# Adding the experts' results to the residual rows in DRAM by accumulating scatters

## The chip, the cores and the metric

The kernel runs on one core of a Trainium2 chip. The metric is the device time of one execution in microseconds (us). Before the change it was 1234.18 us, the median of 3 runs (1233.81 to 1234.71).

## The reference, cut to what matters

One decoder layer on 1024 tokens of width 1024, all in float32. A mixing layer (dilated attention and a convolution) gives `x1`; then a mixture of experts adds to it, and a last norm gives the output:

```python
x = x + gt1 * mix                                   # x1
h2 = rms_norm(x, g_norm2) * (1.0 + sc2) + sh2
x = x + gt2 * hier_moe(h2, ...)                     # 32 experts, each token goes to 2 of them
return rms_norm(x, g_final)

# hier_moe, per token t and its two experts e:
#   out[t] += w[t, e] * ((silu(h2[t] @ w_gate[e]) * (h2[t] @ w_up[e])) @ w_down[e])
```

So 2048 rows of 1024 float32 (4 KB each) come out of the experts, two for each token, and each token's two rows are added to its row of `x1` before the last norm.

## The kernel before, in words

The first half of the kernel (up to about 590 us) computes the modulation, the projections, the convolution, the attention, the output projection and the router. In `second_norm` each block of 128 tokens writes its normed rows to the DRAM tensor `h2d` and its residual rows to the DRAM tensor `x1d` (L799, L800). `tables` (L869) turns the router's choice into columns of indices: `ti` is the token of each slot of an expert, `si` is the row of the result buffer of that slot (twice the token, plus 0 or 1 for the token's first or second expert), and `ws` is the weight. Slots that are empty get an index out of bounds, and no row is moved for them.

The second half works through the experts in order. Each has 6 MB of weights (`gate`, `up`, `down`, 2 MB each), loaded by the SP queue (`stage_w`, `eload`, L598) in two 1 MB loads for each into a ring of eight 2 MB buffers, in order of use; a load waits until the buffer's last reader is done. For an expert of 128 slots, `stage_gu` splits each weight into a high and a low part (the ACT cast L931 and the VectorE subtraction L932) and multiplies in three passes (L997 to L999), `stage_h` transposes, and `stage_d` multiplies by `down` (L1065 to L1067). The twelve experts of `PK` have 64 slots and use plain float32 matmuls on the loaded weights (`gu_halves` L977, `d_halves` L1043). One expert, `XP`, is computed for a second block of slots as well. That makes 33 blocks.

GpSimd's queue (POOL) carries, in program order, an indirect DMA that gathers a block's rows of `h2d` (`gather`, L918, into one of three buffers `xe`) and an indirect DMA that scatters a block's results (`scatter`, L1029). VectorE writes the results, scaled by `ws` and `gt2`, into one of two buffers `ys` (L1049, L1073). In the kernel before, each result has its own row of a DRAM buffer `ybuf` of 2048 rows, and the scatters are declared free of each other, so that none waits for the one ahead of it.

Behind the experts stands `overflow(0)`: a conditional block (`tc.If`, L1245) for slots that did not fit, on all engines. In this run it is skipped. Then comes the end, a loop over eight blocks of 128 tokens (L1264 to L1278): load both result rows of each token (1 MB a block), add them on GpSimd (L101, called from L1271), add `x1` on VectorE (L1272; `x1d` was loaded ahead of the conditional block, L1237), square and sum on ACT (L1274), root and reciprocal (L1275, L1276), scale (L1277), and store (L1278, issued by ACT). What sets the order of instructions on each engine is the program order with a scheduler that moves ready work forward; each engine and each queue runs its own instructions in order.

Of the kernel before, what the change touches and what calls it, by code (L numbers as in the profile page):

```python
# [9 lines left out]
F32 = mybir.dt.float32  # L10
# [8 lines left out]
T = 1024  # L19
D = 1024  # L20
H = 8
E = 32
# [23 lines left out]
def trunk_kernel(ctx, tc, x, c, w_mod, b_mod, g_norm1, w_in, conv_w, conv_b, conv_ln_g, conv_ln_b,  # L46
# [13 lines left out]
    dram = ctx.enter_context(tc.tile_pool(name="dram", bufs=1, space=DRAM))  # L60

    h2d = dram.tile([T, D], F32, name="h2d")
    ybuf = dram.tile([2 * T, D], F32, name="ybuf")
    x1d = dram.tile([T, D], F32, name="x1d")
    modd = dram.tile([4, D], F32, name="modd")

# [514 lines left out]
    def ring(i):  # L581

        i %= NR
        if i not in rings:
            if i < 5:
                rings[i] = (raw if i < 2 else rawl if i == 2 else mixp).tile([P, 8, 512], F32, name="raw")
            else:
                rings[i] = (wop if i > 5 else att0).tile([P, 8, 512], F32, name="raw", tag=("pT0", "wo6", "wo2")[i - 5])
        return rings[i]
# [248 lines left out]
    for tt in range(2, 8):  # L838
# [3 lines left out]
        if tt % 4 == 3:  # L842
# [11 lines left out]
    wop0.release()  # L854


    early_t, late_t = [[rtc.tile([P, n], dt, name=f"{nm}{n}") for nm, dt in (("ti", I32), ("si", I32), ("ws", F32))]
                       for n in (LO, E - LO + 1 + NOV)]

    half_t = [rtc.tile([P, E - LO], dt, name=f"{nm}h") for nm, dt in (("ti", I32), ("si", I32), ("ws", F32))]  # L860
    tb = rtc.tile([P, 4, 2, E], F32, name="tb")

    def slots(e):

        if e < LO:
            return [t[:, e:e + 1] for t in early_t]
        return [t[:, e - LO:e - LO + 1] for t in (half_t if e in PK else late_t)]

    def tables(tb, dst, pool, halves=False):  # L869

        ti, si, ws = dst
        n = tb.shape[-1]
        em = pool.tile([P, n], F32, name=f"em{n}", bufs=1)
        v.tensor_scalar(em, tb[:, 0, :], 0.0, BIG, op0=OP.is_equal, op1=OP.mult)
        if halves:
            v.scalar_tensor_tensor(em, tb[:, 0, :], -1.0, em, op0=OP.add, op1=OP.add)
            v.tensor_scalar(ti, em, 2.0, upper, op0=OP.mult, op1=OP.add)
            v.scalar_tensor_tensor(em, em, 2.0, tb[:, 1, :], op0=OP.mult, op1=OP.add)
            v.tensor_scalar(si, em, 2.0, upper, op0=OP.mult, op1=OP.add)
        else:  # L880
            v.scalar_tensor_tensor(ti, tb[:, 0, :], -1.0, em, op0=OP.add, op1=OP.add)
            v.scalar_tensor_tensor(em, tb[:, 0, :], -1.0, em, op0=OP.add, op1=OP.add)
            v.scalar_tensor_tensor(si, em, 2.0, tb[:, 1, :], op0=OP.mult, op1=OP.add)
        v.tensor_add(ws, tb[:, 2, :], tb[:, 3, :])

    t0 = wk3.tile([P, 4, LO], F32, name="t0", bufs=1)
# [21 lines left out]
          for i in range(NX)]  # L908
    for t in xe:
        nc.gpsimd.memset(t, 0.0)  # L910
    scat = []

    gat = []

    def gather(e):
# [110 lines left out]
        st["t", e] = hh, hl  # L1026

    def scatter(ys, e, n):
        s = nc.gpsimd.indirect_dma_start(  # L1029
            out=ybuf.rearrange("t (n f) -> (t n) f", n=n),  # L1030
            out_offset=bass.IndirectOffsetOnAxis(ap=slots(e)[1], axis=0),
            in_=ys, in_offset=None, bounds_check=2 * n * T - 1, oob_is_err=False)
        for o in scat:
            tc.declare_no_dep(s.ins, o.ins, reason="each slot has its own row")
        scat.append(s)

    def d_halves(e):
        h2 = st.pop(("t", e))
        wd = wt[e, 2].rearrange("p (k a) f -> p k (a f)", a=2)
        py = psx.tile([P, D], F32, name="py")[:, 0:512]  # L1040
        for k in range(4):
            for g in range(2):
                nc.tensor.matmul(py[64 * g:64 * g + 64, :], h2[:, k % 2, k // 2 * 64:k // 2 * 64 + 64],  # L1043
                                 wd[:, k, 512 * g:512 * g + 512], start=(k == 0), stop=(k == 3),
                                 skip_group_check=True)
        ys = moe.tile([P, D], F32, name="ys")[:, 0:512]
        for g in range(2):
            ps = slice(64 * g, 64 * g + 64)
            nc.vector.scalar_tensor_tensor(ys[ps], py[ps], slots(e)[2][ps], gt2b[ps, 512 * g:512 * g + 512],  # L1049
                                           op0=OP.mult, op1=OP.mult)  # L1050
        scatter(ys, e, 2)

    def stage_d(*es):
        if es[0] in PK:
            return d_halves(es[0])
        hs = [st.pop(("t", e)) for e in es]
        wd = wt[es[0], 2]
        py = psx.tile([P, D], F32, name="py")
        py = [[py[:, 0:512], py[:, 512:1024]]]
        if len(es) > 1:  # L1060
            py.append([psg.tile([P, F], F32, name=nm) for nm in ("pg", "pu")])
        for k, hi, lo in wparts(wd, DP):
            for (hh, hl), o2 in zip(hs, py):
                for half, o in enumerate(o2):
                    nc.tensor.matmul(o, hh[:, k, :], hi[:, half, :], start=(k == 0), stop=False)  # L1065
                    nc.tensor.matmul(o, hh[:, k, :], lo[:, half, :], start=False, stop=False)  # L1066
                    nc.tensor.matmul(o, hl[:, k, :], hi[:, half, :], start=False, stop=(k == 3))  # L1067
        for e, o2 in zip(es, py):
            ws = slots(e)[2]
            ys = moe.tile([P, D], F32, name="ys")  # L1070
            for half, o in enumerate(o2):
                sl = slice(half * 512, half * 512 + 512)
                nc.vector.scalar_tensor_tensor(ys[:, sl], o, ws, gt2b[:, sl], op0=OP.mult, op1=OP.mult)  # L1073
            scatter(ys, e, 1)
# [156 lines left out]
    stage_w(E)  # L1231
    stage_d(E - 1)


    fx = [ring(i).rearrange("p (t k) f -> p t (k f)", k=2) for i in (0, 1)]
    for i, f in enumerate(fx):
        nc.sync.dma_start(f, x1d[i * 512:i * 512 + 512, :].rearrange("(t p) d -> p t d", p=P))  # L1237
    gfb = ring(7).rearrange("p k f -> p (k f)")[:, 0:D]
    bcast(gfb, g_final[None, :])

# [19 lines left out]
    psx.release()  # L1260


    yv = ybuf.rearrange("(t k) d -> t (k d)", k=2)
    for tt in range(8):  # L1264
        ts = slice(tt * P, (tt + 1) * P)
        if tt % 2 == 0:
            fy = ring((5, 6, 2, 3)[tt // 2]).rearrange("p (t k a) f -> p t k (a f)", t=2, k=2)
        f = fx[tt // 4][:, tt % 4, :]
        y = fy[:, tt % 2]
        nc.sync.dma_start(y.rearrange("p k d -> p (k d)"), yv[ts, :])  # L1270
        gp(y[:, 0, :], y[:, 0, :], y[:, 1, :], OP.add)  # L1271
        nc.vector.tensor_add(f, f, y[:, 0, :])  # L1272
        fs = moe.tile([P, 2], F32, name="fst")
        nc.scalar.activation(y[:, 1, :], f, AF.Square, accum_out=fs[:, 0:1])  # L1274
        nc.scalar.activation(fs[:, 1:2], fs[:, 0:1], AF.Sqrt, scale=1.0 / D, bias=epsc)  # L1275
        nc.vector.reciprocal(fs[:, 1:2], fs[:, 1:2])  # L1276
        nc.vector.scalar_tensor_tensor(y[:, 0, :], f, fs[:, 1:2], gfb, op0=OP.mult, op1=OP.mult)  # L1277
        nc.scalar.dma_start(out[ts, :], y[:, 0, :])  # L1278
    moe.release()
    tabp.release()  # L1280
    wop.release()
# [57 lines left out]
```

## Time and profile before

| | before |
|---|---|
| median of 3 runs | 1234.18 us |
| the profiled execution | 1230.17 us |
| its span in the trace | 1228.4 us |
| granted TensorE clock, mean | 0.951 |
| busy share PE, DVE, ACT, POOL | 89%, 68%, 43%, 17% |
| DMA moved | 301.03 MB, mean 245 GB/s |

All times below are from the one profiled execution, counted from the start of its span. A row of the timeline gives start, duration, engine, line, operation, what is written and read, and in brackets how long the engine was idle before it and what ended that. An engine name with a q is the sequencer of that engine, which issues DMAs and waits on semaphores.

### The profile page before, as it was taken

What the parts mean: (1) busy time and instruction counts of PE and PEld (TensorE: products, weight loads), DVE (VectorE), ACT (ScalarE), POOL (GpSimd) and SP (SyncE); (2) the same over time, 40 slices, a digit from 0 to 9 for tenths busy, and PEclk for the clock granted to TensorE, in tenths of its full rate; (3) what the DMA queues carried; (4) which work ended last, traced back from release to release, by engine and by line L of the source; (5) the groups of instructions that cost most, each with busy time, mean ns of one, the idle gap of its engine ahead of it and who ended that gap; (6) DMA issues with size and microseconds to landing.
All of it is one profiled execution on the core that took longest, in us unless ns stands there. A gap on an engine that the chain in (4) does not pass through costs nothing. (4 is left out here: it accounts for less than half of the span.)

```text
span 1228.4 us, 16007 instructions
## 1 busy us (share of the span) xinstructions
PE 1095.8 (89%) x5838; PEld 800.0 (65%) x5838; DVE 832.1 (68%) x1344; ACT 533.7 (43%) x818; POOL 214.5 (17%) x197
## 2 busy tenths in 40 slices
PE   4899999998999999999599999999999999998910
PEld 0667777786566667888477787777757666665700
DVE  1458999993664567676698997667543566567538
ACT  1431111114777654222475775556432354455412
POOL 2340000005221105001301112121110111100044
PEclk8799999998999999999799999999999999999965
DMA  9542634202001018538697999999999999999265
GB/s 367 185 155 85 224 121 154 103 6 81 20 16 36 1 73 298 207 137 311 215 326 279 352 380 391 419 420 416 419 399 364 404 361 387 414 346 367 111 243 209
DMA packets 61244, 301.03 MB, mean 245 GB/s; under 512 B 11840, under 2 KB 16192, under 8 KB 32484
## 3 DMA queue, kind: packets, MB, share of 16 engines
q1 hardware_dynamic: 49076, 261.55, 55.2%
q0 software_dynamic: 10656, 34.17, 7.8%
q10 hardware_dynamic: 1424, 4.20, 0.9%
q8 instruction: 48, 0.79, 0.3%
q14 instruction: 40, 0.33, 0.1%
HBM read 284.66 MB, written 26.76 MB: 254 GB/s over the span
## 5 line engine op out<-in xcount | busy, mean ns | idle before, releaser
L932 DVE TENSOR_TENSOR elo<-raw,ehi 128x1024 fp32r<-128x1024 f32 x240 | 287.1, 1221 | 48.0 <-ACT ehi L931 44.2
L931 ACT CAST ehi<-raw 128x1024 fp32r<-128x1024 f32 x240 | 249.1, 1050 | 93.8 <-PE pg L999 44.4
L320 DVE SCALAR_TENSOR_TENSOR cv<-cv,cwT 128x1024 f32<-128x1024 f32 x120 | 154.1, 1284 | 3.6
L272 PE MATMUL pb<-hT,whi 128*128 128x512 f32 x256 | 101.0, 394 | 1.7 <-POOL hT L101 1.3
L271 PE MATMUL pb<-hT,whi 128*128 128x512 f32 x256 | 102.1, 400 | 0.0
L273 PE MATMUL pb<-hT,wlo 128*128 128x512 f32 x256 | 100.4, 393 | 0.0
L998 PE MATMUL pg<-elo,xh 128*128 128x512 f32 x168 | 70.5, 420 | 7.9 <-DVE elo L932 7.9
L997 PE MATMUL pg<-ehi,xh 128*128 128x512 f32 x168 | 69.7, 416 | 5.2 <-ACT ehi L931 4.5
L999 PE MATMUL pg<-ehi,xl 128*128 128x512 f32 x168 | 69.1, 411 | 0.0
L998 PE MATMUL pu<-elo,xh 128*128 128x512 f32 x168 | 66.9, 398 | 1.4 <-DVE elo L932 1.4
L1066 PE MATMUL py<-elo,hh 128*128 128x512 f32 x160 | 65.6, 410 | 2.6 <-DVE elo L932 2.6
L997 PE MATMUL pu<-ehi,xh 128*128 128x512 f32 x168 | 66.0, 393 | 1.4 <-ACT ehi L931 1.4
L999 PE MATMUL pu<-ehi,xl 128*128 128x512 f32 x168 | 65.6, 391 | 0.0
L1065 PE MATMUL py<-ehi,hh 128*128 128x512 f32 x160 | 64.4, 403 | 0.1
L1067 PE MATMUL py<-ehi,hl 128*128 128x512 f32 x160 | 63.4, 396 | 0.0
L271 PEld LDWEIGHTS pb<-hT,whi 128*128 128x128 f32 x256 | 48.3, 189 | 21.8 <-ACT whi L105 9.2
L1029 POOL DMA_INDIRECT ybuf<-ys,si x21 | 26.2, 1247 | 180.8 <-DVE ys L1073 179.2
L272 PEld LDWEIGHTS pb<-hT,whi 128*128 128x128 f32 x256 | 48.2, 188 | 13.0 <-POOL hT L101 2.9
L918 POOL DMA_INDIRECT xe<-h2d,ti x21 | 27.2, 1296 | 162.3 <-PE pt L965 110.7
L273 PEld LDWEIGHTS pb<-hT,wlo 128*128 128x128 f32 x256 | 48.2, 188 | 10.4 <-DVE wlo L108 0.6
L425 ACT ACTIVATE ns<-ns,st 128x128 f32<-128x128 f32 (+7 forms) x64 | 49.3, 773 | 9.2 <-DVE st L421 8.7
L421 DVE CUSTOM_DVE_ANT_0 ns<-sc,raw 128x384 f32<-128x384 f32 (+5 forms) x64 | 33.1, 535 | 24.7 <-PE sc L418 13.9
(293 smaller groups left out, 2254.5 us busy)
## 6 DMA issues: line engine op xcount, KB each, us to landing
raw<-in_w_exp_gate_dram SPq DMA_DIRECT2D x64, 1024.0 KB
raw<-in_w_exp_up_dram SPq DMA_DIRECT2D x64, 1024.0 KB
raw<-in_w_exp_down_dram SPq DMA_DIRECT2D x64, 1024.0 KB
wm<-in_w_mod_dram POOLq DMA_DIRECT2D x16, 1024.0 KB, 5.0
wm<-in_w_mod_dram SPq DMA_DIRECT2D x8, 1024.0 KB
raw<-ybuf SPq DMA_DIRECT2D x8, 1024.0 KB
raw<-in_w_in_dram SPq DMA_DIRECT2D x3, 2048.0 KB
xt<-in_x_dram SPq DMA_DIRECT2D x8, 512.0 KB
```

Source lines behind the costliest of these rows:

```text
L271: nc.tensor.matmul(p[half], hi[:, k, :], hT[0][:, k, sl], start=(k == 0), stop=False)
L272: nc.tensor.matmul(p[half], hi[:, k, :], hT[1][:, k, sl], start=False, stop=False)
L273: nc.tensor.matmul(p[half], lo[:, k, :], hT[0][:, k, sl], start=False, stop=(k == 7))
L320: nc.vector.scalar_tensor_tensor(y, u[:, j:j + T], w, y, op0=OP.mult, op1=OP.add)
L931: nc.scalar.copy(hi, src)
L932: (nc.gpsimd if i == pool else nc.vector).tensor_tensor(lo, src, hi.bitcast(F32), op=OP.subtract)
L997: nc.tensor.matmul(o, xh[:, k, :], hi[:, kk, :], start=(k == 0), stop=False)
L998: nc.tensor.matmul(o, xh[:, k, :], lo[:, kk, :], start=False, stop=False)
L999: nc.tensor.matmul(o, xl[:, k, :], hi[:, kk, :], start=False, stop=(k == 7))
L1065: nc.tensor.matmul(o, hh[:, k, :], hi[:, half, :], start=(k == 0), stop=False)
L1066: nc.tensor.matmul(o, hh[:, k, :], lo[:, half, :], start=False, stop=False)
L1067: nc.tensor.matmul(o, hl[:, k, :], hi[:, half, :], start=False, stop=(k == 3))
```

## The change

`ybuf`, the index column `si` and the free order of the scatters go. A scatter now adds its rows to the rows of `x1d` in DRAM (`compute_op=OP.add`), with the token index `ti`; since any two scatters may meet in a row, each waits for the landing of the one ahead of it. The end loads only `x1d`, now behind the last scatter, 512 KB a block, and forms the reciprocal root on GpSimd by `rstd_of` (L94).

```diff
-    ybuf = dram.tile([2 * T, D], F32, name="ybuf")
...
     def tables(tb, dst, pool, halves=False):
-        ti, si, ws = dst
+        ti, ws = dst
...
             v.tensor_scalar(ti, em, 2.0, upper, op0=OP.mult, op1=OP.add)
-            v.scalar_tensor_tensor(em, em, 2.0, tb[:, 1, :], op0=OP.mult, op1=OP.add)
-            v.tensor_scalar(si, em, 2.0, upper, op0=OP.mult, op1=OP.add)
         else:
             v.scalar_tensor_tensor(ti, tb[:, 0, :], -1.0, em, op0=OP.add, op1=OP.add)
-            v.scalar_tensor_tensor(em, tb[:, 0, :], -1.0, em, op0=OP.add, op1=OP.add)
-            v.scalar_tensor_tensor(si, em, 2.0, tb[:, 1, :], op0=OP.mult, op1=OP.add)
...
     def scatter(ys, e, n):
-        s = nc.gpsimd.indirect_dma_start(
-            out=ybuf.rearrange("t (n f) -> (t n) f", n=n),
-            out_offset=bass.IndirectOffsetOnAxis(ap=slots(e)[1], axis=0),
-            in_=ys, in_offset=None, bounds_check=2 * n * T - 1, oob_is_err=False)
-        for o in scat:
-            tc.declare_no_dep(s.ins, o.ins, reason="each slot has its own row")
-        scat.append(s)
+        nc.gpsimd.indirect_dma_start(
+            out=x1d.rearrange("t (n f) -> (t n) f", n=n),
+            out_offset=bass.IndirectOffsetOnAxis(ap=slots(e)[0], axis=0),
+            in_=ys, in_offset=None, bounds_check=n * T - 1, oob_is_err=False, compute_op=OP.add)
...
-    fx = [ring(i).rearrange("p (t k) f -> p t (k f)", k=2) for i in (0, 1)]
-    for i, f in enumerate(fx):
-        nc.sync.dma_start(f, x1d[i * 512:i * 512 + 512, :].rearrange("(t p) d -> p t d", p=P))
     gfb = ring(7).rearrange("p k f -> p (k f)")[:, 0:D]
     bcast(gfb, g_final[None, :])
...
-    yv = ybuf.rearrange("(t k) d -> t (k d)", k=2)
     for tt in range(8):
         ts = slice(tt * P, (tt + 1) * P)
-        if tt % 2 == 0:
-            fy = ring((5, 6, 2, 3)[tt // 2]).rearrange("p (t k a) f -> p t k (a f)", t=2, k=2)
-        f = fx[tt // 4][:, tt % 4, :]
-        y = fy[:, tt % 2]
-        nc.sync.dma_start(y.rearrange("p k d -> p (k d)"), yv[ts, :])
-        gp(y[:, 0, :], y[:, 0, :], y[:, 1, :], OP.add)
-        nc.vector.tensor_add(f, f, y[:, 0, :])
-        fs = moe.tile([P, 2], F32, name="fst")
-        nc.scalar.activation(y[:, 1, :], f, AF.Square, accum_out=fs[:, 0:1])
-        nc.scalar.activation(fs[:, 1:2], fs[:, 0:1], AF.Sqrt, scale=1.0 / D, bias=epsc)
-        nc.vector.reciprocal(fs[:, 1:2], fs[:, 1:2])
-        nc.vector.scalar_tensor_tensor(y[:, 0, :], f, fs[:, 1:2], gfb, op0=OP.mult, op1=OP.mult)
-        nc.scalar.dma_start(out[ts, :], y[:, 0, :])
+        y = ring(2 + tt // 2).rearrange("p (t k a) f -> p t k (a f)", t=2, k=2)[:, tt % 2]
+        f, q = y[:, 0, :], y[:, 1, :]
+        nc.sync.dma_start(f, x1d[ts, :])
+        fs = moe.tile([P, 1], F32, name="fst", bufs=4)
+        nc.scalar.activation(q, f, AF.Square, accum_out=fs)
+        r = rstd_of(moe, fs, 1, 1.0 / D)
+        nc.vector.scalar_tensor_tensor(q, f, r, gfb, op0=OP.mult, op1=OP.mult)
+        nc.scalar.dma_start(out[ts, :], q)
```

First place: GpSimd's queue around expert `XP` and its second block, whose scatters stand closest together. `xe` is a gather, `ybuf` or `x1d` a scatter; DMASW names the semaphores of GpSimd's own DMAs (eight in turn), DVE is VectorE's, PE TensorE's. Before:

```order
L918 DMA xe_4872<-h2d,ti_4833 128x1024 [waits DMASW7_49,PE_49]
L1029 DMA ybuf<-ys,sih 4096x512 [waits DMASW4_49,DVE_49]
L1029 DMA ybuf<-ys,sih 4096x512 [waits DVE_49]
L918 DMA xe_4870<-h2d,tih 128x512 [waits DMASW6_49,DMASW0_49,PE_49]
L1029 DMA ybuf<-ys,si_4834 2048x1024 [waits DVE_49] x2
L918 DMA xe_4871<-h2d,ti_4833 128x1024 [waits DMASW2_49,DMASW1_49,PE_49]
```

And now:

```order
L911 DMA xe_4866<-h2d,ti_4831 128x1024 [waits DMASW7_49,PE_49]
L1023 DMA x1d<-ys,tih 2048x512 [waits DMASW1_49,DVE_49]
L1023 DMA x1d<-ys,tih 2048x512 [waits DMASW4_49,DVE_49]
L911 DMA xe_4864<-h2d,tih 128x512 [waits DMASW0_49,PE_49]
L1023 DMA x1d<-ys,ti_4831 1024x1024 [waits DMASW5_49,DVE_49]
L1023 DMA x1d<-ys,ti_4831 1024x1024 [waits DMASW7_49,DVE_49]
L911 DMA xe_4865<-h2d,ti_4831 128x1024 [waits DMASW2_49,PE_49]
```

Nothing is moved here: the same gathers and scatters stand in the same places. Each scatter has gained a wait on the semaphore of the scatter ahead of it, and what stands behind it in the queue waits with it.

Second place: the SP queue from the last weight load to the conditional block. HW names the semaphores of the loads. Before:

```order
L598 DMA raw<-in_w_exp_down_dram 128x2048 [waits DMAHW1_49,DVE_49]
L1237 DMA raw<-x1d 128x4x1024 [waits DMAHW2_49,PE_49]
L1237 DMA raw<-x1d 128x4x1024 [waits DMAHW3_49,DVE_49]
L521 DMA raw<-in_g_final_dram 128x1024 [waits DMAHW4_49,DMAHW0_49,PE_49]
L1242 TENSOR_LOAD pos [waits DVE_49]
L1245 COMPARE_AND_BRANCH
```

And now:

```order
L597 DMA raw<-in_w_exp_down_dram 128x2048 [waits DMAHW1_49,DVE_49]
L1229 TENSOR_LOAD pos [waits DVE_49]
L1229 ISA x2
L520 DMA raw<-in_g_final_dram 128x1024 [waits DMAHW2_49,DMAHW0_49,PE_49]
L1232 COMPARE_AND_BRANCH
```

The two 2 MB loads of `x1d` have left this place; the weight loads ahead of it are the same. Behind the conditional block eight loads of `x1d` (L1254) now stand where eight of `ybuf` (L1270) stood.

Third place: ACT behind the conditional block, at the end of the kernel. Before:

```order
L1274 ACTIVATE raw,fst<-raw 128x1024
L1275 ACT_TABLE_LOAD
L1275 ACTIVATE fst<-fst,epsc 128x1
L1274 ACTIVATE raw,fst<-raw 128x1024
L1275 ACTIVATE fst<-fst,epsc 128x1
L1278 DMA out_dram<-raw 128x1024 x2
L1274 ACTIVATE raw,fst<-raw 128x1024
L1275 ACTIVATE fst<-fst,epsc 128x1
```

And now:

```order
L1256 ACTIVATE raw,fst<-raw 128x1024 x2
L1259 DMA out_dram<-raw 128x1024
L1256 ACTIVATE raw,fst<-raw 128x1024
L1259 DMA out_dram<-raw 128x1024
L1256 ACTIVATE raw,fst<-raw 128x1024
L1259 DMA out_dram<-raw 128x1024
L1256 ACTIVATE raw,fst<-raw 128x1024
```

The roots are gone from ACT, and the square of block n+2 stands behind the store of block n.

## Rows read from the trace of the kernel before

**Rows 1.** Stages: us; busy (x) of PE, PEld, DVE, ACT, POOL; clock; DMA share; GB/s.
```profile
740.00:880.00 140.00, 140.00 (x790) 101.60 (x788) 95.07 (x99) 74.84 (x90) 27.27 (x19) 1.00 1.01 415
...
960.00:1130.00 170.00, 157.09 (x790) 109.40 (x786) 110.91 (x115) 87.05 (x104) 20.99 (x17) 0.98 0.98 384
...
1181.30:1228.40 47.10, 0.00 (x0) 0.00 (x0) 32.40 (x24) 12.62 (x25) 23.77 (x8) 0.50 0.67 268
```

**Rows 2.** What SP's weight loads waited for, 640 to 1130 us: total, times, longest.
```profile
SPq L598 <- DVE elo L932: 195.5, 79, 4.9
...
SPq L598 <- DMA raw<-in_w_exp_up_dram: 29.9, 14, 3.1
```

**Rows 3.** Timeline, expert 15: its gate weights issued by SP, and first read.
```profile
815.59 3.13 SPq L598 DMA_DIRECT2D raw<-in_w_exp_gate_dram  x2
...
847.07 1.05 ACT L931 CAST ehi<-raw 128x1024 fp32r<-128x1024 f32 x1 [0.25 <-PE pu L999]
```

**Rows 4.** Timeline of POOL, gathers and scatters.
```profile
745.30 1.03 POOL L918 DMA_INDIRECT xe<-h2d,tih  x1 [6.98 <-PE pt L965]
...
766.09 1.02 POOL L1029 DMA_INDIRECT ybuf<-ys,sih  x1 [10.54 <-DVE ys L1049]
...
781.22 1.74 POOL L1029 DMA_INDIRECT ybuf<-ys,si  x1 [5.17 <-DVE ys L1073]
783.26 1.97 POOL L918 DMA_INDIRECT xe<-h2d,ti  x1 [0.30 <-issue]
```

**Rows 5.** DMA view, 740 to 880 us: GpSimd's queue; issues with median us to landing.
```profile
q0 software_dynamic: 2185, 4.29, 8.0%
...
ybuf<-ys,si POOLq DMA_INDIRECT x5, 9.5
xe<-h2d,ti POOLq DMA_INDIRECT x5, 10.8
```

**Rows 6.** Timeline of the end, from the last two scatters on.
```profile
1169.98 0.97 POOL L1029 DMA_INDIRECT ybuf<-ys,si  x1 [13.32 <-DVE ys L1073]
...
1173.50 1.51 DVE L1049 SCALAR_TENSOR_TENSOR ys<-py,wsh,gt2b 64x512 f32<-64x512 f32 x2 [3.79 <-PE py L1043]
1175.29 0.99 POOL L1029 DMA_INDIRECT ybuf<-ys,sih  x1 [4.34 <-DVEq L1245]
1181.46 13.23 SPq L1270 DMA_DIRECT2D raw<-ybuf  x8
1186.40 2.33 POOL L101 TENSOR_TENSOR raw<-raw 128x1024 f32<-128x1024 f32 x1 [10.13 <-DMA raw<-ybuf]
...
1223.14 1.73 ACTq L1278 DMA_DIRECT2D out_dram<-raw  x2
```

**Rows 7.** Line 1245, skipping the conditional block: ns min/median/max, when.
```profile
L1245 POOLq INC_SWDGE_SEM  x1: 2067/2067/2067, 1179.2 to 1179.2; - x1
```

**Rows 8.** DMA view, 1175 to 1182 us: GpSimd's queue (packets, MB, share).
```profile
q0 software_dynamic: 80, 0.23, 8.5%
```

**Rows 9.** Costliest groups from 1181.3 us on: busy, mean ns; idle before, releaser.
```profile
L101 POOL TENSOR_TENSOR raw<-raw 128x1024 f32<-128x1024 f32 x8 | 23.8, 2999 | 10.9 <-DMA raw<-ybuf 10.9
...
L1272 DVE TENSOR_TENSOR raw<-raw 128x1024 f32<-128x1024 f32 x8 | 15.9, 2020 | 16.0 <-POOL raw L101 16.0
L1274 ACT ACTIVATE raw<-raw 128x1024 f32<-128x1024 f32 x8 | 8.4, 1053 | 41.6 <-DVE raw L1272 30.6 <-DMA out_dram<-raw 11.1
```

**Rows 10.** Timeline of the second norm: square, reciprocal root on POOL, scaling.
```profile
510.42 1.06 ACT L783 ACTIVATE h<-xr 128x1024 f32<-128x1024 f32 x1 [3.48 <-issue]
511.38 0.19 ACT L783 ACTIVATION_READ_ACCUMULATOR h<-xr 128x1 f32 x1
511.65 0.19 POOL L96 TENSOR_SCALAR rstd<-ss 128x1 f32<-128x1 f32 x1 [19.45 <-ACT h L783]
511.93 0.54 POOL L97 TENSOR_TENSOR rstd<-rstd,mhalf 128x1 f32<-128x1 f32 x1
512.50 1.28 DVE L797 SCALAR_TENSOR_TENSOR h<-xr,rstd,a2b 128x1024 f32<-128x1024 f32 x1 [2.17 <-POOL rstd L97]
```

More of the change, by code (lines that the diff above doesn't have):

```diff
@@ L854, in trunk_kernel @@
     wop0.release()
-    early_t, late_t = [[rtc.tile([P, n], dt, name=f"{nm}{n}") for nm, dt in (("ti", I32), ("si", I32), ("ws", F32))]
+    early_t, late_t = [[rtc.tile([P, n], dt, name=f"{nm}{n}") for nm, dt in (("ti", I32), ("ws", F32))]
                        for n in (LO, E - LO + 1 + NOV)]
-    half_t = [rtc.tile([P, E - LO], dt, name=f"{nm}h") for nm, dt in (("ti", I32), ("si", I32), ("ws", F32))]
+    half_t = [rtc.tile([P, E - LO], dt, name=f"{nm}h") for nm, dt in (("ti", I32), ("ws", F32))]
     tb = rtc.tile([P, 4, 2, E], F32, name="tb")
@@ L910, in trunk_kernel @@
         nc.gpsimd.memset(t, 0.0)
-    scat = []
     gat = []
@@ L1048, in d_halves @@
             ps = slice(64 * g, 64 * g + 64)
-            nc.vector.scalar_tensor_tensor(ys[ps], py[ps], slots(e)[2][ps], gt2b[ps, 512 * g:512 * g + 512],
+            nc.vector.scalar_tensor_tensor(ys[ps], py[ps], slots(e)[1][ps], gt2b[ps, 512 * g:512 * g + 512],
                                            op0=OP.mult, op1=OP.mult)
@@ L1068, in stage_d @@
         for e, o2 in zip(es, py):
-            ws = slots(e)[2]
+            ws = slots(e)[1]
             ys = moe.tile([P, D], F32, name="ys")
```

## The prediction

> **What bounds the kernel now.** I read the busy times by stage first. From 740 to 880 us, among the experts, TensorE is busy in all 140 us and the DMA engines in all of them too (share 1.01, 415 GB/s); from 960 to 1130 us TensorE is busy in 157 of 170 us and DMA still at 0.98, 384 GB/s; from 1181.3 us to the end, 47.1 us, TensorE does nothing, DMA is busy at 0.67 and VectorE in 32.4 us [rows 1]. So there are two stages to settle: one in which two resources look full, and an end of 47 us that is a pipeline of its own.
>
> In the first, which of the two is late last? The waits of SP answer: its weight loads wait above all for VectorE to finish with a buffer of the ring (195.5 us in 79 waits), and far less for a DMA (29.9 us in 14 waits for one of the three weight tensors, the other two being like it) [rows 2]. The loads are mostly held back by the readers. A single weight shows the lead: expert 15's gate is issued by 818.7 us and first read by ACT at 847.07 us, 28.4 us later [rows 3]. At most eight loads of 1 MB stand in SP's queue (it waits for the one eight back), so at 415 GB/s [rows 1] a load lands within 8 x 1.05 MB / 415 GB/s = 20.2 us of its issue. The lead of this weight, in the fullest stretch, is at least 8 us. TensorE sets the pace, and DMA has a small reserve.
>
> At the end [rows 6], the last scatter is issued at 1175.29 us. GpSimd waits for its landing, then runs an instruction of 2.07 us for the skipped block, from 1179.2 us [rows 7], and SP's first load goes out at 1181.46 us. The first block is worked on from 1186.40 us; the stores end with the span at 1228.4 us. That is 46.9 us from the first load. In it 8 additions on GpSimd take 3.0 us each, 23.8 us, VectorE's additions 2.0 us each, and ACT stands idle 30.6 us for VectorE [rows 9].
>
> **The change, part by part.**
>
> *The end.* The first load is 512 KB and not 1 MB: first block ready 1186.40 - 1181.46 = 4.9 us after issue, less 0.52 MB / 415 GB/s = 1.3 us, so 3.7 us. GpSimd's and VectorE's additions go. What is left of a block is a square (1.05 us [rows 9] and 0.19 us to read the sum), GpSimd's two instructions and a scaling. The same three steps in the second norm [rows 10]: the square starts at 510.42 us, the scaling at 512.50 us and takes 1.28 us, so 2.08 + 1.28 = 3.4 us from the start of a square to the end of the scaling, and a store after it, whose issue I put at 0.34 us, an estimate from the two issues in 1.73 us at the end of rows 6. ACT runs the square of block n+2 behind the store of block n, so two blocks go round in 3.4 + 0.1 + 0.34 = 3.8 us. The stores of blocks 0, 2, 4 and 6 are issued at 3.5, 7.3, 11.1 and 14.9 us after the first landing, that of block 7 1.5 us later (a square and a scaling behind), at 16.4 us. From the issue of the last store to the end of the span: the last two issues cover 1223.14 to 1224.87 us [rows 6], the last starting 0.34 us before that, so 1228.4 - 1224.53 = 3.9 us. Sum: 3.7 + 16.4 + 3.9 = 24.0 us; 0.5 us more for loads and stores that now cross on the DMA engines (8.4 MB at 415 GB/s is 20.2 us of work in it), 24.5 us. The saving is 46.9 - 24.5 = **22.4 us**. The bounds: 20 us of DMA work and the two ends of about 4 us could make 28 us of it; 23 us if the squares run ahead.
>
> *The accumulating scatter itself.* No row shows one. The nearest are a plain scatter and a gather. A 4 KB row of the last scatter costs 8.5% of 16 engines x 7 us = 9.5 us of engine time for 0.23 MB, 56 rows, so 0.17 us a row [rows 8]. Accumulating reads the old row as well. From below a row costs as before; from above I take a gather and a scatter in sequence, 0.34 us. I take the upper end, since both moves have to be made. In the stretch of 740 to 880 us GpSimd's queue moved 4.29 MB [rows 5], half of it scatters, since each row that is gathered is scattered later: 2.1 MB, 524 rows. Extra work: 524 x 0.17 / 16 = 5.6 us on every engine, and the lead of at least 8 us covers it. From 960 to 1130 us the rate is 384 and not 415 GB/s [rows 1], which leaves room for (415 - 384) / 415 x 170 = 13 us more. All scatters but the last four fall among the weight loads, about 1800 rows, 1800 x 0.17 / 16 = 19 us against 8 + 13 = 21 us of cover. So in the expert stage I cost it at **0 us**; with no cover it is 19 us, which would eat the gain. Bounds 0 and 14 us.
>
> The Trainium skill bears on that choice ("Collectives: The Full Stack", section "The bandwidth ceiling: the fold count and why AG ≠ RS ≠ AR"): a sum made by the DMA engines costs no cycles for the addition but needs two source reads on the same ring, and ran at half the rate of a copy. By it the row costs 0.34 us too, and the sum stays; no row here shows an accumulating packet.
>
> *The wait of each scatter for the one ahead.* Behind a waiting scatter on GpSimd's queue stand gathers, and for these TensorE waits, three blocks later. A plain scatter lands 9.5 us after issue in the full stretch [rows 5], and scatters follow each other in about 15 us (766.09, 781.22 us [rows 4]). A landing of up to 15 us costs nothing. Gathers have room too: a buffer is refilled at 745.30 us and read empty just before 783.26 us, 38 us, of which landing takes 10.8 us, so 27 us. Only where scatters follow closely does the wait show: the pair of `XP` delays what is behind it by about a landing, inside those 27 us. Cost 0; bounds 0 and 3 us.
>
> *At the last scatter* this wait has no cover. The one ahead is issued at 1169.98 us, the last could go at 1175.29 us [rows 6], 5.3 us later. Plain, a scatter lands within 3.9 us here (1175.29 to 1179.2 us, rows 6 and 7). With two moves to a row and the same start-up I take 5.4 us, between 3.9 and 7.8 (twice). So 0.1 us of wait, to which I add 0.9 us for the loads of `g_final` that share the engines; bounds 0 and 2.5 us. Its own landing is on the path: **+1.5 us**, bounds 0 and 3.9. Together +2.5 us.
>
> *The rest* costs nothing: eight small VectorE instructions of the tables are gone, most of them behind the first gathers, and the two loads of `x1d` that SP issued among the last experts; there the loads come after the last weight, so no weight gets earlier. ACT's table load goes with the root (it lay in the saved end).
>
> **Sum:** -22.4 + 2.5 = -19.9 us, on the profiled execution 1230.2 - 19.9 = 1210.3 us. That execution was 4.0 us below the median of the runs (1234.18 us); against the median I predict **1214 us**.
>
> **Rivals.**
>
> *Weights come late (slower).* Place: the expert stage, 640 to 1130 us, TensorE waiting for weights. If an accumulating row takes much longer than a plain gather and scatter together, for instance six times a plain row (0.85 us more), the 1800 rows cost 1800 x 0.85 / 16 = 96 us on each engine; less the 21 us of cover the weights come 75 us late, and with the 19.9 us gained the time is 1289 us. It decides from the point where the lateness is 20 us: 41 us of extra work, 0.36 us a row more, rows of three times the plain length. For it: DMA share 1.0 in rows 1. Against: 28 us between issue and use in rows 3, in the fullest stretch.
>
> *Some of that.* Rows of two and a half times the length, 0.25 us more, 28 us of work against 21: 7 us lost, 1221 us. Landings over 15 us that push the gathers back by more than their 27 us would look alike.
>
> *The end stays bound by DMA or by the chain on ACT.* If loads and stores hinder each other as the 28 us bound says, and the last landing takes its upper bound: 3.5 + 3.9 us more than I took, about 1221 us. For it: DMA is already at 0.67 in the end before [rows 1], which is to be half as long with 8.4 MB of its 12.6 MB left. Against: 20.2 us of work still fit into 24.5.
>
> *The change buys nothing.* If the skipped block, and not the loads, set the start of each engine's part of the end, the end would shrink little: 1234 us. Against: in the end the engines wait for loads and each other [rows 9].
>
> **How the numbers follow.** My forecast 0.65, own range 1208 to 1218 us (the bounds of the last wait and landing, and the end a little better or worse); end bound by DMA 0.12; some weights late 0.12; no gain 0.02; slower 0.09. A measurement of this kernel can tell about 0.2%, 2.5 us, from no change. Faster by more: 0.65 + 0.12 + 0.09 of the partly late = 0.86; within 0.2%: 0.03 of the partly late and the 0.02 of no gain, 0.05; slower 0.09. The range takes in the two middle rivals, with a little below my own: 1206 to 1228 us.
>
> **What would show it.** Right: TensorE's work ends where it did (about 1173 us), SP's first load of `x1d` is issued between 1182 and 1185 us, the end then takes 23 to 26 us, ACT's squares follow each other in pairs of 3.8 us, and the scatters land in under 15 us. Wrong: idle TensorE before the first products of an expert with a weight load as releaser, or scatters whose distance is their landing; then the rows were mis-sized. If the end is longer than 28 us, its pipeline was misread.

## The result and the profile after

The changed kernel took **1218.96 us** (median of 4 runs, 1218.07 to 1220.17) against 1233.99 us for the kernel before (4 runs, 1232.48 to 1234.71): a ratio of 0.988, with an interval of 0.9863 to 0.9898. That is 15.0 us gained where 19.9 us were forecast. Timed again beside other kernels it had 1220.09 us and a ratio of 0.9898 (0.9881 to 0.9915). The question is where 5 us went.

Two profiles of the changed kernel are at hand. In the first (span 1218.4 us) TensorE's last matmul ends at 1177.96 us, in the second (span 1213.7 us) at 1173.60 us. In the profile before it was at 1169.80 + 3.65 = 1173.45 us:

```profile
1169.80 3.65 PE L1043 MATMUL py<-raw,h 128*64 128x512 f32 x16 [1.55 <-issue]
```

The 4.5 us of the first profile are hardly the change's: TensorE's 2000th matmul, ahead of everything that the change touches, starts 3.9 us later in it than before (417.1 and 413.2 us), and in the second profile 0.1 us later. So all that follows is read from the last matmul on, or from the second profile, whose TensorE ends where it did before.

The stages of the first profile of the changed kernel, which answer to [rows 1], with the same columns.

```profile
740.00:880.00 140.00, 140.00 (x791) 101.99 (x791) 99.50 (x105) 75.95 (x92) 29.93 (x19) 1.00 1.02 400
960.00:1130.00 170.00, 157.09 (x805) 110.72 (x802) 109.59 (x114) 86.96 (x104) 27.38 (x18) 0.97 1.00 385
1193.20:1218.40 25.20, 0.00 (x0) 0.00 (x0) 10.28 (x8) 9.21 (x16) 7.49 (x16) 0.50 0.87 334
```

TensorE is as busy among the experts as it was: 140.00 of 140 us, 157.09 of 170 us. The end is 25.2 us from SP's first load, not 46.9. Now what lies between: the timeline of the second profile, POOL, SP and DVE, from the last scatter but one on (start, duration, engine, line, what, idle time ahead and its releaser).

```profile
1170.12 1.55 POOL L1023 DMA_INDIRECT x1d<-ys,ti  x1 [12.74 <-DVE ys L1064]
...
1171.06 0.34 SPq L520 DMA_DIRECT2D raw<-in_g_final_dram  x1
...
1173.64 1.51 DVE L1040 SCALAR_TENSOR_TENSOR ys<-py,wsh,gt2b 64x512 f32<-64x512 f32 x2 [3.79 <-PE py L1034]
...
1182.03 1.57 POOL L1023 DMA_INDIRECT x1d<-ys,tih  x1 [10.36 <-issue]
...
1188.60 4.95 SPq L1254 DMA_DIRECT2D raw<-x1d  x8
```

VectorE has the last results ready at 1173.64 + 1.51 = 1175.15 us, and the scatter is issued at 1182.03 us, 6.9 us later. In [rows 6] the same steps are 0.3 us apart. From that scatter to SP's first load it is 6.57 us, where it was 6.17 us before. So the second profile differs from the one before as follows: TensorE's end comes 0.1 us later, the last scatter stands 6.6 us later behind it and the load 0.4 us later behind that, and the end takes 25.1 instead of 46.9 us, 21.8 less. The sum is -14.7 us, which is the difference of the two spans; the medians differ by 15.0 us. Both executions lie some 4 us below the median of their kernel's runs, so the two differences agree.

The expert stage shows where the accumulating rows went. GpSimd's queue and its landings from 740 to 880 us (DMA view of the first profile: packets, MB, share; median us to landing), which answer to [rows 5], and SP's waits from 640 to 1130 us (total, times, longest), for [rows 2] (here the gate's and the up tensor's rows).

```profile
q0 software_dynamic: 2336, 4.05, 11.4%
...
x1d<-ys,ti POOLq DMA_INDIRECT x6, 11.6
...
x1d<-ys,tih POOLq DMA_INDIRECT x4, 8.7
```

```profile
SPq L597 <- DVE elo L925: 106.1, 56, 4.5
SPq L597 <- DMA raw<-in_w_exp_gate_dram: 80.1, 37, 3.5
...
SPq L597 <- DMA raw<-in_w_exp_up_dram: 75.5, 37, 4.1
```

The queue takes 11.4% of the engines' time instead of 8.0, which is 4.8 us more on each of them in 140 us (5.6 forecast). SP's loads now wait 106 us for VectorE instead of 195.5, and 75 to 80 us for each of the weight tensors instead of 30: much of the reserve of the DMA engines has been spent, though TensorE doesn't wait for weights yet.

The end of the first profile: two blocks of the pipeline, all engines, and the last stores.

```profile
1203.86 0.32 POOL L95 TENSOR_SCALAR rstd<-fst 128x1 f32<-128x1 f32 x1 [1.05 <-ACT raw L1256]
...
1204.62 1.06 ACT L1256 ACTIVATE raw<-raw 128x1024 f32<-128x1024 f32 x1 [0.85 <-POOL rstd L95]
1204.85 1.29 DVE L1258 SCALAR_TENSOR_TENSOR raw<-raw,rstd 128x1024 f32<-128x1024 f32 x1 [0.72 <-POOL rstd L96]
...
1206.17 0.34 ACTq L1259 DMA_DIRECT2D out_dram<-raw  x1
...
1206.61 1.06 ACT L1256 ACTIVATE raw<-raw 128x1024 f32<-128x1024 f32 x1 [0.83 <-POOL rstd L95]
...
1208.61 1.06 ACT L1256 ACTIVATE raw<-raw 128x1024 f32<-128x1024 f32 x1 [0.85 <-POOL rstd L95]
...
1212.18 2.34 ACTq L1259 DMA_DIRECT2D out_dram<-raw  x2
```

A square stands behind each store, and two blocks take 1208.61 - 1204.62 = 4.0 us, as the loop of the prediction says with 3.8.

### The profile page after: what moved, and what is told of

Same layout as the page of the kernel before. It is cut to its first block, busy times and chain, and to the rows that moved or that the text cites. A ratio compares the mean times of both kernels' runs of the same rounds, so it can differ in the third digit from the quotient of the medians.

```text
span 1218.4 us, 15998 instructions
## 1 busy us (share of the span) xinstructions
PE 1099.1 (90%) x5838; PEld 801.9 (66%) x5838; DVE 809.3 (66%) x1320; ACT 530.8 (44%) x809; POOL 216.4 (18%) x205
## 5 line engine op out<-in xcount | busy, mean ns | idle before, releaser
L1023 POOL DMA_INDIRECT x1d<-ys,ti x21 | 38.4, 1828 | 185.1 <-DVE ys L1064 173.6
L270 PEld LDWEIGHTS pb<-hT,whi 128*128 128x128 f32 x256 | 48.3, 189 | 21.8 <-ACT whi L104 9.2
L272 PEld LDWEIGHTS pb<-hT,wlo 128*128 128x128 f32 x256 | 48.2, 188 | 10.4 <-DVE wlo L107 0.6
L424 ACT ACTIVATE ns<-ns,st 128x128 f32<-128x128 f32 (+7 forms) x64 | 49.4, 774 | 11.5 <-DVE st L420 11.1
```

The costliest lines, as they stand in the source:

```text
L270: nc.tensor.matmul(p[half], hi[:, k, :], hT[0][:, k, sl], start=(k == 0), stop=False)
L272: nc.tensor.matmul(p[half], lo[:, k, :], hT[0][:, k, sl], start=False, stop=(k == 7))
```

## The experiments

**The wait alone, in the kernel before.**

```diff
-        for o in scat:
-            tc.declare_no_dep(s.ins, o.ins, reason="each slot has its own row")
-        scat.append(s)
```

> The kernel before with the wait alone: each scatter into ybuf waits for the one ahead, nothing is added by a DMA. Theory A (the wait costs nothing among the experts, only at the last scatter, where a plain one lands in 4.8 us and GpSimd needs 1.7 us behind it): the last two stand 6.5 us apart instead of 5.3, 1235 us, no change that can be told. Rival D (the waits hold up gathers, and TensorE with them): 1238 us or more, and TensorE waits for xe.

1232.43 us (12 runs) against 1231.59 us (17 runs), ratio 1.0001 (0.9983 to 1.0018). Its last two scatters (POOL's timeline):

```profile
1171.92 0.98 POOL L1029 DMA_INDIRECT ybuf<-ys,si  x1 [13.36 <-DVE ys L1070]
1177.23 0.99 POOL L1029 DMA_INDIRECT ybuf<-ys,sih  x1 [4.33 <-DVEq L1242]
```

They are 5.31 us apart, as before, and the first lands in 4.5 us (DMA view from 1168 to 1176 us). Theory A holds, though its 6.5 us at the last scatter were too many; D falls: with plain rows the wait is free, in the stage and at the end.

**Plain rows, with the waits.**

```diff
-            in_=ys, in_offset=None, bounds_check=n * T - 1, oob_is_err=False, compute_op=OP.add)
+            in_=ys, in_offset=None, bounds_check=n * T - 1, oob_is_err=False)
```

> The changed kernel with scatters that overwrite the rows of x1 instead of adding to them (the addition of the experts' results is left out); every wait stays. Theory A (the 5 us that are missing went into the wait of the last scatter for the one ahead, 12.2 us between the two against 5.3 before, of which only the packets' own time depends on the addition): a 4 KB row takes 0.16 us instead of 0.33, the two stand about 10.5 us apart, and about 2 us come back: 1217 us. Rival B (the dearer rows themselves cost it, in the expert stage too): all 5 us come back and TensorE's work ends earlier by some us: 1213 to 1214 us.

1216.26 us, ratio 0.9886 (0.9856 to 0.9915). POOL and SP, and the DMA view from 1173 to 1186 us:

```profile
1175.01 0.98 POOL L1023 DMA_INDIRECT x1d<-ys,ti  x1 [13.36 <-DVE ys L1064]
1180.32 0.99 POOL L1023 DMA_INDIRECT x1d<-ys,tih  x1 [4.33 <-DVEq L1232]
...
1186.10 4.92 SPq L1254 DMA_DIRECT2D raw<-x1d  x8
```

```profile
x1d<-ys,ti POOLq DMA_INDIRECT x1, 4.1
```

The wait is gone altogether (5.31 us apart again), and the load comes 7.6 us behind the last matmul (1178.49 us) instead of 15.0. Theory A had the place right but not the split: it gave the addition 2 us of the wait, and without the addition none of it is left. Rival B falls: TensorE's work does not end earlier. The time shows less than the trace, since this profile's span ends 4.2 us after the last store's packets where that of the changed kernel ends 1.6 us after; what that is stays open.

**The load of `g_final` out of the way.**

```diff
-    gfb = ring(7).rearrange("p k f -> p (k f)")[:, 0:D]
+    gfb = ring(0).rearrange("p k f -> p (k f)")[:, 0:D]
```

> The changed kernel with the load of g_final into ring buffer 0, free since expert 28, instead of buffer 7, which the last weight holds: its 0.5 MB moves out of the time of the last two scatters. Theory A (its packets hold up the last scatter but one, which starts 5.2 us after its issue where an undisturbed one starts after 2.1): the last two stand 9 us apart instead of 12.2, 3 us come back: 1216 us. Rival C (4 to 5 us to the first packet is the scatter's own, as it is among the weight loads): no change, 1219 us.

1215.64 us, ratio 0.9873 (0.9848 to 0.9899). POOL and SP:

```profile
1173.66 1.55 POOL L1023 DMA_INDIRECT x1d<-ys,ti  x1 [12.74 <-DVE ys L1064]
1181.69 1.57 POOL L1023 DMA_INDIRECT x1d<-ys,tih  x1 [6.49 <-issue]
...
1188.20 6.42 SPq L1254 DMA_DIRECT2D raw<-x1d  x8
```

8.0 us apart instead of 12.2 (first profile) and 11.9 (second); the load 11.1 us behind the last matmul (1177.14 us). Theory A holds, C falls. The landing itself, from the DMA view of the changed kernel and then of this one, 1173 to 1186 us:

```profile
q0 software_dynamic: 144, 0.44, 17.3%
...
x1d<-ys,ti POOLq DMA_INDIRECT x1, 10.4
```

```profile
x1d<-ys,ti POOLq DMA_INDIRECT x1, 6.3
```

So of 10.4 us of landing, 4.1 are a plain scatter's, 2.2 the addition's, and 4.1 the load's that goes ahead of it. The packets' start times in the trace say how: in the changed kernel the scatter's first packet starts 5.2 us after issue, behind `g_final`'s; with the early load 2.1 us; with plain rows 1.6 us, ahead of `g_final`'s (2.4 us), although that is loaded at the same place. This fits the time that the issue takes on GpSimd, 0.98 us for a plain scatter and 1.55 for an adding one. The first fence also prices the rows: 17.3% of 16 engines x 13 us = 36 us for 108 rows, **0.33 us a row** against 0.17 [rows 8]. That price is not the same everywhere: with the early load, when the scatter has the DMA engines to itself, the packets of the same 108 rows take 48.3 us in the trace, 0.45 us a row. The reason is not shown.

**The last scatter without a wait.** It goes into a DRAM buffer `xz` that nobody reads.

```diff
-            out=x1d.rearrange("t (n f) -> (t n) f", n=n),
+            out=(xz if e == E - 1 else x1d).rearrange("t (n f) -> (t n) f", n=n),
```

> The changed kernel with the last expert's scatter going into a buffer of its own that is never read (the last expert's addition is left out), so that it waits for nothing. Theory A (the wait of the last scatter is the missing 5 us): the last scatter is issued about 1.8 us behind the last matmul instead of 8.7, SP's first load of x1 comes about 6 us earlier, 1213 us. Rival B (the dearer rows in the expert stage cost it): no change, 1219 us.

1215.41 us, ratio 0.9874 (0.9843 to 0.9904).

```profile
1176.59 1.55 POOL L1024 DMA_INDIRECT x1d<-ys,ti  x1 [12.74 <-DVE ys L1065]
1182.08 1.57 POOL L1024 DMA_INDIRECT xz<-ys,tih  x1 [3.94 <-DVEq L1233]
...
1189.53 5.21 SPq L1255 DMA_DIRECT2D raw<-x1d  x8
```

5.5 us apart, and the load 9.5 us behind the last matmul (1180.07 us) instead of 15.2: 5.8 us less, the size that A gave. The times alone would tell neither this run nor the two before it from the changed kernel, since the intervals of the ratios overlap; the reading rests on the traces. In this execution TensorE ended late.

**The changed kernel again** (no edit).

> The changed kernel once more, unchanged, timed beside the next three on the same chip, so that these can be set against it. If the last wait is a property of the kernel and not of the one execution profiled, the last two scatters stand 12 us apart again, and the first load of x1 comes 15 us behind the last matmul; the end takes 25 us from there.

1220.09 us; the rows are shown above: 11.9 us apart, the load 15.0 us behind the last matmul, the end 25.1 us. All three repeat.

**Two edits that the order on the engines undid.** To put TensorE's work between the last two results, expert 31's products were written ahead of expert 30's; to take the stores off ACT, they were given to SP. The diff has the second edit; the first, which reorders `stage_d` and `d_halves`, is left out.

```diff
-        nc.scalar.dma_start(out[ts, :], q)
+        nc.sync.dma_start(out[ts, :], q)
```

> The changed kernel with g_final loaded early into ring buffer 0 and, besides, expert 31 (the half-row one) brought ahead of expert 30's down products, so that 6 us of TensorE's work stand between the last two scatters' results. Theory A (the last scatter waits for the one ahead): the first of the two is issued 6 us earlier, lands before the results of the second are there, and SP's first load of x1 comes 8 to 9 us behind the last matmul, against 15.2 in the changed kernel and 11.1 with the early load alone: 1216.5 - 6.5 = 1210 us beside 1216.5 for the changed kernel. Rival E (the time between the last matmul and the load is the last scatter's own landing and the skipped block): 11 us again, 1213 us.

> The changed kernel with the eight stores of the result issued by SP instead of ACT, so that no square stands behind a store. Theory F (the end runs at the pace of the loop square, root, scaling, store, square on ACT, 4.0 us for two blocks): squares follow the loads, 1.3 us apart, and the end shrinks from 25.2 to about 22 us, where 20 us of transfers bound it; 3 us less than the changed kernel. Rival G (the transfers bound it already, DMA share 0.87 in these 25 us): under 1 us less.

> All three together: g_final early, expert 31 ahead of expert 30's down products, stores issued by SP. If A and F hold, 6.5 and 3 us add up: about 9 us less than the changed kernel; if E and G hold instead, 4 to 5 us less.

1220.2 us (0.9909, 0.9886 to 0.9932), 1225.54 us (0.9933, 0.9918 to 0.9947) and 1228.83 us (0.9957, 0.9942 to 0.9973). None tests its theory. In the first, expert 31's copy on ACT stayed behind four casts, its products ran last as ever, and its scatter was issued at 1177.18 us, the other 7.0 us after it. In the second, SP's timeline shows what the scheduler made of loads and stores on one queue:

```profile
1192.06 1.87 SPq L1254 DMA_DIRECT2D raw<-x1d  x4
1199.06 6.35 SPq L1259 DMA_DIRECT2D out_dram<-raw  x4
1205.49 2.18 SPq L1254 DMA_DIRECT2D raw<-x1d  x4
```

Four loads stand behind four stores, each of which waits for a scaling; the end takes 31.6 us. The third has both faults.

**The half-row expert ahead**, done by the table of the experts instead.

```diff
-PK = (7, 9, 11, 13, 16, 17, 19, 20, 23, 25, 28, 31)
+PK = (7, 9, 11, 13, 16, 17, 19, 20, 23, 25, 28, 30)
...
-    gfb = ring(7).rearrange("p k f -> p (k f)")[:, 0:D]
+    gfb = ring(0).rearrange("p k f -> p (k f)")[:, 0:D]
```

> The changed kernel with g_final loaded early into ring buffer 0, and with the twelfth half-row place moved from expert 31 to expert 30, so that the last scatter but one is the half-row one and expert 31's full down products stand behind it on TensorE. (The edit of the run named for the swap was meant to do this and did not: the scheduler left expert 31's copy on ACT behind four casts, and TensorE ran expert 30 first as before.) Theory A: a half-row scatter needs 7 us until the next one can be issued, TensorE's work between the two results takes 7 to 9, so the last scatter waits 0 to 1 us; it needs 7.9 us until SP's first load, so that comes 9.6 to 10.5 us behind the last matmul, against 15.0 in the changed kernel and 11.1 with the early load alone: 4.5 to 5.5 us less than the changed kernel. Rival E (something else holds the load): 11 us or more behind the last matmul.

**1212.48 us**, ratio 0.9843 (0.9805 to 0.9881), the lowest median of the study.

```profile
1167.62 1.55 POOL L1023 DMA_INDIRECT x1d<-ys,tih  x1 [13.89 <-DVE ys L1040]
1179.63 1.57 POOL L1023 DMA_INDIRECT x1d<-ys,ti  x1 [10.46 <-DVEq L1232]
...
1187.78 5.21 SPq L1254 DMA_DIRECT2D raw<-x1d  x8
```

The last scatter goes out 1.9 us behind the last matmul (1177.72 us), with VectorE and not the landing ahead of it; the load 10.1 us behind that matmul. A holds; what is left is a full scatter's own 8.2 us. By the times this is not told apart from the changed kernel beyond doubt: the interval just touches that of its second timing from below, and overlaps that of the first. In the trace the load is 4.9 to 5.2 us earlier behind the last matmul.

**The end: stores on SP behind all loads; then the roots with eight buffers too.**

```diff
+    with tc.high_priority():
+        for tt in range(8):
+            nc.sync.dma_start(ys[tt][:, 0, :], x1d[tt * P:(tt + 1) * P, :])
...
-        nc.scalar.dma_start(out[ts, :], q)
+        nc.sync.dma_start(out[ts, :], q)
```

> The changed kernel with the stores of the result on SP, now behind all eight loads on that queue (in the run before this the scheduler put four stores ahead of four loads, and the end took 31.6 us). Theory F: squares follow the loads 1.3 us apart, the end shrinks from 25.1 to about 22 us, where 20 us of transfers bound it. Rival G (transfers bound it already): 24.5 to 25 us.

> The kernel with the early g_final load and the half-row expert ahead, whose load of x1 came 10.1 us behind the last matmul, with an end in which SP issues all eight loads and then the stores, and the small tiles of the sums and roots have eight buffers. Theory K (the end's step of 2.0 us a block is the loop of GpSimd and VectorE: with two buffers for the root GpSimd begins the next root as VectorE begins a scaling, and its first instruction then takes 1.3 us instead of 0.2; ACT's stores were not it): with the roots worked out ahead, scalings follow each other 1.3 to 1.5 us apart and the end takes about 23 us instead of 25.1 to 25.6, bound by 20 us of transfers: 2 us less than the kernel with the two edits alone, 1210.5 us where that had 1212.5. Rival G (transfers bound the end already): scalings stay 2 us apart or wait for loads, 25 us, 1212.5 us.

The first, on the changed kernel: 1219.81 us (0.9904, 0.9866 to 0.9942), an end of 25.6 us. The second, on the kernel with the half-row expert ahead and with `bufs=8` for `rstd` and `fst`: 1214.6 us (0.9862, 0.9837 to 0.9888), an end of 25.0 us. F falls, and so does the remedy of K. POOL and DVE in the second:

```profile
1200.20 1.28 DVE L1260 SCALAR_TENSOR_TENSOR raw<-raw,rstd 128x1024 f32<-128x1024 f32 x1 [0.72 <-POOL rstd L96]
1200.24 1.28 POOL L95 TENSOR_SCALAR rstd<-fst 128x1 f32<-128x1 f32 x1
...
1201.61 0.55 POOL L96 TENSOR_TENSOR rstd<-rstd,mhalf 128x1 f32<-128x1 f32 x1
...
1202.20 1.29 DVE L1260 SCALAR_TENSOR_TENSOR raw<-raw,rstd 128x1024 f32<-128x1024 f32 x1 [0.72 <-ACT raw L1258]
```

ACT's squares run ahead, yet scalings are still 2.0 us apart. GpSimd's first root instruction, on 128 numbers, takes as long as VectorE's scaling beside it and ends with it; the second follows, and only then the next scaling. More buffers don't help, since GpSimd does not get on while VectorE scales: the loop that K named is there, but it does not hang on the buffers. So two loops have the same step of 2.0 us a block, the one over ACT's stores and the one between GpSimd and VectorE, and taking one away leaves the other. Rival G is not shown by this: transfers are at 0.87 to 0.89 of the end. A root off GpSimd was not tried.

**Each result scattered twice.**

`xz` is a second DRAM buffer, of the size of `x1d`.

```diff
+        nc.gpsimd.indirect_dma_start(
+            out=xz.rearrange("t (n f) -> (t n) f", n=n),
+            out_offset=bass.IndirectOffsetOnAxis(ap=slots(e)[0], axis=0),
+            in_=ys, in_offset=None, bounds_check=n * T - 1, oob_is_err=False, compute_op=OP.add)
```

> The changed kernel with each result scattered twice: once more, also added, into a DRAM buffer that nobody reads. This doubles the cost of the accumulating rows, 2048 x 0.33 us / 16 = 42 us more on each DMA engine, nearly all of it among the weight loads. If the cover in the expert stage is the 21 us that the prediction worked out, of which the change has used 19, TensorE waits for weights and its last matmul comes 35 to 40 us later, near 1213 us, and the time is 1255 to 1260 us. Rival H (the weights' lead is far greater than 8 us over most of the stage, the cover is at least 60 us): TensorE's last matmul stays where it is, and only the last landings cost 3 to 6 us: 1225 us.

1255.45 us, ratio 1.0185 (1.0155 to 1.0214). TensorE's last matmul ends at 1213.38 us. One of its stages, SP's waits from 640 to 1130 us, and one of ACT's from 640 to 1180 us:

```profile
740.00:880.00 140.00, 127.94 (x713) 91.64 (x710) 88.23 (x93) 66.43 (x82) 42.95 (x26) 0.96 0.99 359
```

```profile
SPq L598 <- DMA raw<-in_w_exp_up_dram: 109.6, 38, 4.5
...
SPq L598 <- DVE elo L926: 68.8, 28, 4.5
```

```profile
ACT ehi L925 <- DMA raw<-in_w_exp_down_dram: 28.0, 9, 13.5
```

TensorE, busy all the time from 740 to 880 us before, now stands idle 12 us there. It is the weights that come late: ACT waits 28.0 us for those of `down` (4.5 us in the first profile of the changed kernel), while TensorE waits for no gather but the first, 6.6 us, as in the changed kernel. The added DMA work is some 40 us on each engine up to TensorE's last matmul (packets' times in the trace), and that matmul ends 35.4 us later than in the first profile, whose 2000th matmul starts at much the same time (416.8 us here, 417.1 there). So the changed kernel had some 5 us of cover left, and the rival with late weights does happen once the rows cost twice as much. H falls.

## Why the prediction came out as it did

*The end: right, and a little too short.* 24.5 us were forecast, 25.2 and 25.1 measured. By its terms, in the first profile: first block 3.5 us behind the load (3.7), last store issued at 1212.18 + 2.34 - 0.34 = 1214.18 us, 17.5 us after the first square (16.4), then 4.2 us (3.9). The loop of two blocks is 4.0 instead of 3.8 us, mainly because GpSimd's first instruction takes 0.32 and not 0.19 us; and the last store stands 2.0 and not 1.5 us behind the one ahead, by the loop of GpSimd and VectorE, which the prediction did not have. The end is the term that made the gain: -21.8 of -22.4 us.

*The accumulating row: right where other transfers run beside it.* 0.34 us taken, 0.33 measured there, 0.45 for a scatter alone. The rule cited there from the Trainium skill ("Collectives: The Full Stack", section "The bandwidth ceiling: the fold count and why AG ≠ RS ≠ AR"), half the rate of a copy, agrees with the first of these, 0.33 against 0.17 us, and not with the second.

*The cover: right in the outcome, and close.* 19 us of added work against 21 of cover were to cost nothing, and TensorE's work ends 0.1 us later in the second profile. Both sizes were too low: by the packets' times the added work is 22 us on each engine up to TensorE's last matmul, and the doubled scatter leaves some 5 us more of cover, so about 27 in all. That 22 us still fitted was not in the prediction's numbers, by which the weights would have been 1 us late.

*The waits among the experts: right.* Landings of 11.6 and 8.7 us, under the 15 between scatters. Only the pair of `XP` is held to the landing, as the prediction said: in the first profile its scatters are 10.9 us apart (958.39 and 969.30 us) at a landing of 10.2, and TensorE waits for no gather there.

*The wait of the last scatter: wrong, and this is the missing 5 us.* The step was: the one ahead lands in 5.4 us, the last could go 5.3 us behind it, "So 0.1 us of wait, to which I add 0.9 us for the loads of `g_final`". It waits 6.6 us longer than before. Three things were mis-sized. The landing was worked out from a plain scatter of half rows with the engines otherwise idle, with twice the time for the rows; a full adding one needs 6.3 us. The load of `g_final`, priced as a share of the engines, goes ahead of it as a whole, 4.1 us. And behind the landing another 1.7 us pass until the next scatter is issued, which had no term at all: in the first profile the two are 12.2 us apart at a landing of 10.4, with the early load 8.0 at 6.3. What fills the 1.7 us is not shown; it is no fixed price, since 0.7 us were enough at the pair of `XP`, and 0.8 in the kernel before with the waits (5.31 us apart at a landing of 4.5). The bound of 2.5 us, too, was 4.1 us short. *The last landing itself* was dearer by 0.4 and not 1.5 us: its landing grew, but the skipped block's instruction took 1.21 us instead of 2.07 [rows 7], for a reason that stays open (first profile: ns min, median, max, and when):

```profile
L1232 POOLq INC_SWDGE_SEM  x1: 1207/1207/1207, 1191.7 to 1191.7; - x1
```

Sum: +6.6 and +0.4 for the +2.5 forecast, and 0.6 us less saved at the end: 5.1 us, about the distance between 1214 and 1218.96 us. SP's first load came at 1188.60 and 1193.20 us, not between 1182 and 1185: of the signs listed as right, that one failed, and with it the scatters' distance at the last pair, which is the landing and what follows it.

*The rivals.* Late weights did not come, but were near. The end bound by DMA or by ACT, with the last landing at its upper bound, had the time nearly right (1221 us) for the wrong reason: the end kept its length, and the wait ahead of it grew. Its sum was wrong as well: of the landing's bound of 3.9 us, 1.5 were in the forecast already, so it comes to about 1220 us.

## What to carry to other kernels

A wait that is free inside a pipeline is not free at its last step, where nothing covers it: work out that step with the landing of the very transfer that is waited for (full size, its own operation), plus the time that the engine needs behind the landing, and ask which transfers are issued just behind it. A small load that can go anywhere should not be issued in the middle of the last chain. And before an end is sped up by freeing one engine, look for a second loop with the same step.

## What the runs showed of the hardware

An adding indirect DMA occupies GpSimd 1.55 us at the last scatters where a plain one takes 0.98. Its first packet starts 2.1 us behind issue and not 1.6, and it came behind a load issued by SP 0.9 us after it, which a plain one came ahead of.

A plain scatter of half rows moved two of them in one packet, an adding one each by itself: the 108 half rows that leave in 54 packets of 4 KB at 1132.21 us before leave in 108 packets of 2 KB at 1137.86 us in the first profile.

GpSimd is held up beside VectorE's scaling, which reads two tiles. The root's first instruction takes 0.19 us alone [rows 10] and 1.28 beside a scaling. The Trainium skill ("SBUF — State Buffer", section "Who interferes with whom") says that a VectorE instruction with two inputs in SBUF, the on-chip memory of the tiles, contends with a GpSimd instruction that reads SBUF; the trace agrees. A gather's issue may suffer likewise. With the small VectorE instructions of the tables gone, a 3.5 us group of subtractions begins 0.4 us ahead of the experts' first gather, which takes 1.90 us; before, the gather began just ahead of the group and took 1.19 us (POOL, before and then second profile; the last row is the third gather, with none of the group beside it).

```profile
594.20 1.19 POOL L918 DMA_INDIRECT xe<-h2d,ti  x1 [6.46 <-DMA gt2b<-modd]
```

```profile
593.75 1.90 POOL L911 DMA_INDIRECT xe<-h2d,ti  x1 [6.45 <-DMA gt2b<-modd]
...
598.98 1.00 POOL L911 DMA_INDIRECT xe<-h2d,ti  x1 [0.27 <-POOL xe L905]
```

That the subtractions hold it up is not shown: the second gather takes 1.77 and 1.78 us, though they run beside all of it before and beside half of it now. TensorE's wait for the first gather, before and then in the second profile (total, times, longest):

```profile
PE pt L965 <- DMA xe<-h2d,ti: 5.5, 1, 5.5
```

```profile
PE pt L958 <- DMA xe<-h2d,ti: 6.7, 1, 6.7
```

So taking out instructions, which the prediction put at no cost, moved what runs beside them, and TensorE's wait grew by 1.2 us here; its last matmul still ends 0.1 us later than before.
